# A dense expert stage cut in two: all U products first, their gelu parked in DRAM, then all sums over V

## The chip, the cores and the metric

The kernel runs on one core of one Trainium2 chip. The metric is device time in microseconds (us) of one execution. PE is the matrix engine, PEld its weight load, DVE the vector engine, ACT the scalar engine, POOL the GpSimd engine, SP the engine that only issues loads. "Row" below means one of the 128 slices of 128 experts, unless a row of the profile is meant.

## The reference, cut to what matters

A decoder block: a hybrid attention mixer on 16 meta tokens and 512 tokens, then a product-key expert layer (PEER), then a norm. The expert layer is what the change is about:

```python
s1 = jnp.einsum('thd,hkd->thk', q[:, :, 0], sub_keys1)      # 8 heads, 128 keys
s2 = jnp.einsum('thd,hkd->thk', q[:, :, 1], sub_keys2)
v1, i1 = lax.top_k(s1, 16); v2, i2 = lax.top_k(s2, 16)
cand = v1[..., :, None] + v2[..., None, :]
sc, pos = lax.top_k(cand, 16)                               # 16 of 256 pairs
eidx  = (i1 * 128 + i2) at pos                              # 8*16 experts a token
gates = softmax(sc)
act = gelu(einsum('nkd,nd->nk', expert_u[eidx], x), approximate=False)
y   = einsum('nk,nkd->nd', gates * act, expert_v[eidx])     # 16384 experts in all, d = 1024
```

## The kernel before

The 512 tokens are four blocks of 128. Blocks 0 to 2 go through `front(0)` and `mid(0)` (mixer and projections), block 3 through `front(1)` and `mid(1)`. `topk(b)` is the lookup of a block: on DVE, with a few score matmuls ahead of it.

For blocks 0 to 2 the expert layer is **dense**: all 16384 experts are computed, in 128 rows of 128 experts. `u_phase(i1)` loads a 512 KB slice of U (`uf`), splits it into a high part (ACT, `uh`) and a low part (DVE, `ul`), runs 24 matmuls of 384 columns into `pj`, and writes gelu of the result to a slot of `ring`, 24 slots in SBUF that earlier stages left free. `v_operands(i1)` loads a 512 KB slice of V (`vf`), splits it (`vh`, `vl`), multiplies the row's gelu with the gate table `gt` (line 986), splits that (`wh2`, `wl2`), and `v_block` adds 18 matmuls of 512 columns to six accumulators `acc`. The gate table comes from `spread(b)`: for each of the blocks 0 to 2 it builds one-hot matrices on DVE (`ohu`, `ohl`, `B`, lines 861 to 872) and POOL (`Am`), multiplies them on PE (`px`, 32 groups of four products a block, line 878), and stores the result to DRAM (`Gd`), from where `gt` is loaded for eight rows at a time.

Block 3 is **gathered**: for each of 128 pairs per token, POOL issues an indirect load of 128 expert rows from U (512 KB, `gu`), and DVE makes the dot product (`u_dot`, line 827); for each group of 16 pairs it then does the same from V (`v_sum`, line 838). That is 256 gathers and 256 DVE operations.

Two things set the order. A string, `SCHED`, names the steps up to the dense stage: `f` and `m` are steps of `front(1)` and `mid(1)`, `t`/`c` a lookup whole or its first step, `s` a spread, `u` an early U row. After it, U rows fill the ring; then one loop takes one U row (23 ahead) and one V row each pass, with lookup 3 and then `GRATE` = 2.35 gathered steps a pass. The order in the source is a priority; the framework's scheduler places the instructions on each engine, and each engine then runs in that order. U and V loads have two buffers each, gathers have five (`GB`).

## Time and profile before

| | us |
|---|---|
| median of 2 runs | 1719.8 (1718.99 to 1720.6) |
| the profiled execution, its own time | 1722.37 |
| its span, first to last instruction | 1720.6 |
| PE busy in the span | 1608.3 (93%) |
| DVE busy | 1233.7 (72%) |
| moved by DMA | 376.04 MB, mean 219 GB/s |

Sums are made against the span; the median lies 0.8 us below it, and the profiled execution's own time 1.8 us above. A busy PE counts matmuls from start to modelled end, which overlap, so "busy all the time" is read together with how far apart the matmuls start.

### The profile page before, as it was taken

The page shows a single profiled execution, that of the slowest core. Times are in us where ns is not written, and L with a number is a line of the kernel's source. Part 1 is how long each engine was busy: PE and PEld are TensorE (multiplying, and loading weights), DVE is VectorE, ACT ScalarE, POOL GpSimd, SP SyncE. Part 2 cuts the span into 40 slices and gives each one's busy share as a digit, 9 for nine tenths or more (in the row PEclk, how much of TensorE's full clock was granted, in tenths as well). Part 3 has the DMA queues.
Part 4 walks back from the last instruction along what each step waited for, and adds up shares of the span by engine and source line. Part 5 has one row for each costly group of instructions (what it writes and reads, how often), then busy time and mean ns, then how long its engine had stood idle before and what let it go on. Part 6 is the DMA issues. An engine that isn't in the chain of part 4 may idle for free.

```text
span 1720.6 us, 24532 instructions
## 1 busy us (share of the span) xinstructions
PE 1608.3 (93%) x9025; PEld 1432.2 (83%) x9025; DVE 1233.7 (72%) x2484; ACT 704.0 (41%) x1104; POOL 518.2 (30%) x401
## 2 busy tenths in 40 slices
PE   6998998977888789899999999999999999999996
PEld 6957988965577788899999999999999999999875
DVE  4225747489989888978777777777777777777664
ACT  5366365314445456333333333333333333333343
POOL 0020000003345455025334344343444433444310
PEclk9999999999899899999999999999999999999998
DMA  5202125342164345689887887987888888877654
GB/s 172 81 25 86 50 80 172 110 157 102 69 233 165 123 172 203 201 274 369 308 302 283 309 308 281 317 296 289 306 301 292 303 296 299 307 280 279 210 198 133
DMA packets 145705, 376.04 MB, mean 219 GB/s; under 512 B 13712, under 2 KB 63008, under 8 KB 142512
## 3 DMA queue, kind: packets, MB, share of 16 engines
q1 hardware_dynamic: 104112, 211.92, 37.1%
q0 software_dynamic: 36864, 134.23, 21.3%
q10 hardware_dynamic: 4608, 28.31, 4.1%
q8 instruction: 71, 1.16, 0.3%
q14 instruction: 50, 0.41, 0.1%
HBM read 345.03 MB, written 29.36 MB: 218 GB/s over the span
## 4 chain that ended last, share of the span: by engine, by line
PE 79%; DVE 13%; DMA 5%; ACT 2%; issue 1%; POOL 0%; SPq 0%; DVEq 0%; ACTq 0%; POOLq 0%
PE pj L187 12%; PE pj L189 12%; PE pj L188 12%; PE acc L188 9%; PE acc L189 9%; PE acc L187 9%; PE px L878 3%; DVE B L872 2%; PE pk L209 2%; PE pz L373 1%; PE pz L539 1%; DMA vf<-expert_v 1%; PE pz L525 1%; DVE sc L788 1%; DMA wf<-w_out 1%
## 5 line engine op out<-in xcount | busy, mean ns | idle before, releaser
L189 PE MATMUL pj<-xDh,ul 128*128 128x384 f32 x1000 | 338.5, 338 | 5.9 <-DVE ul L183 5.9
L188 PE MATMUL pj<-xDl,uh 128*128 128x384 f32 x1000 | 337.9, 338 | 0.0
L187 PE MATMUL pj<-xDh,uh 128*128 128x384 f32 x1000 | 337.8, 338 | 0.0
L188 PE MATMUL acc<-vl,wh 128*128 128x512 f32 x762 | 298.7, 392 | 1.5 <-DVE vl L183 1.5
L189 PE MATMUL acc<-vh,wl 128*128 128x512 f32 x762 | 298.6, 392 | 0.0
L187 PE MATMUL acc<-vh,wh 128*128 128x512 f32 x762 | 296.3, 389 | 0.4 <-ACT vh L182 0.4
L820 POOL DMA_INDIRECT gu<-expert_u,idx x128 | 183.2, 1431 | 334.4 <-DVE gu L827 193.0
L820 POOL DMA_INDIRECT gu<-expert_v,idx x128 | 178.1, 1392 | 279.3 <-DVE y L838 203.6
L182 ACT ACTIVATE uh<-uf 128x1024 fp32r<-128x1024 f32 x125 | 132.6, 1061 | 300.2 <-PE pj L188 253.6
L874 POOL TENSOR_TENSOR Am<-ohu,ohl 128x512 f32<-128x512 f32 x96 | 129.3, 1367 | 257.0 <-PE pz L530 152.4
L183 DVE TENSOR_TENSOR ul<-uf,uh 128x1024 fp32r<-128x1024 f32 x125 | 157.9, 1263 | 56.2 <-ACT uh L182 56.2
L189 PEld LDWEIGHTS pj<-xDh,ul 128*128 128x128 f32 x1000 | 189.3, 189 | 8.3 <-DVE ul L183 8.1
L187 PEld LDWEIGHTS pj<-xDh,uh 128*128 128x128 f32 x1000 | 189.1, 189 | 4.4 <-ACT uh L182 0.2
L188 PEld LDWEIGHTS pj<-xDl,uh 128*128 128x128 f32 x1000 | 189.3, 189 | 4.1
L188 PEld LDWEIGHTS acc<-vl,wh 128*128 128x128 f32 x762 | 143.0, 188 | 30.6 <-DVE vl L183 2.7
L189 PEld LDWEIGHTS acc<-vh,wl 128*128 128x128 f32 x762 | 143.0, 188 | 29.8
L187 PEld LDWEIGHTS acc<-vh,wh 128*128 128x128 f32 x762 | 143.0, 188 | 28.6 <-ACT vh L182 1.2
L838 DVE SCALAR_TENSOR_TENSOR y<-gu,act,y 128x1024 f32<-128x1024 f32 x128 | 163.8, 1279 | 0.5
L183 DVE TENSOR_TENSOR vl<-vf,vh 128x1024 fp32r<-128x1024 f32 x127 | 154.9, 1220 | 11.2 <-ACT vh L182 11.2
L827 DVE SCALAR_TENSOR_TENSOR gu<-gu,xn 128x1024 f32<-128x1024 f32 x128 | 154.6, 1218 | 0.0
L182 ACT ACTIVATE vh<-vf 128x1024 fp32r<-128x1024 f32 x127 | 133.1, 1048 | 21.1 <-DMA vf<-expert_v 19.8
L878 PE MATMUL px<-Am,B 128*128 128x128 f32 x768 | 102.7, 283 | 26.7 <-DVE B L872 17.1
(365 smaller groups left out, 2458.2 us busy)
## 6 DMA issues: line engine op xcount, KB each, us to landing
vf<-expert_v SPq DMA_DIRECT2D x128, 512.0 KB
uf<-expert_ut SPq DMA_DIRECT2D x125, 512.0 KB
wf<-w_in SPq DMA_DIRECT2D x48, 512.0 KB
Gd<-st ACTq DMA_DIRECT2D x24, 1024.0 KB
gt<-Gd SPq DMA_DIRECT2D x16, 1536.0 KB
wf<-w_out SPq DMA_DIRECT2D x16, 512.0 KB
wf<-w_pq SPq DMA_DIRECT2D x16, 512.0 KB
h<-x SPq DMA_DIRECT2D x4, 512.0 KB
```

What stands on the lines that cost most here:

```text
L182: A.activation(hi, src, AF.Copy)
L183: V.tensor_tensor(lo, src, hi.bitcast(F32), op=OP.subtract)
L187: T.matmul(outp, lh, rh, start=first, stop=False, skip_group_check=True)
L188: T.matmul(outp, lh, rl, start=False, stop=False, skip_group_check=True)
L189: T.matmul(outp, ll, rh, start=False, stop=last, skip_group_check=True)
L209: T.matmul(o, l, r, start=st, stop=sp, skip_group_check=True)
L820: P.indirect_dma_start(out=u, out_offset=None, in_=d[table], in_offset=bass.IndirectOffsetOnAxis(ap=col, axis=0))
L827: V.scalar_tensor_tensor(u, u, 1.0, xns[blk], op0=OP.mult, op1=OP.mult, accum_out=acts[blk][:, k:k + 1]))
L838: V.scalar_tensor_tensor(y, u, acts[blk][:, k:k + 1], y, op0=OP.mult, op1=OP.add))
L872: V.tensor_tensor(B, io4, iT[:, 1, c_].unsqueeze(2).to_broadcast(sh), op=OP.is_equal)
L874: P.tensor_tensor(Am.rearrange("p t (u l) -> p t u l", l=8), ohu[:, l_].unsqueeze(3).to_broadcast([128, 4, 16, 8]), ohl[:, l_].unsqueeze(2 ...
L878: T.matmul(p[:, j * 128:(j + 1) * 128], B[:, j], Am[:, j], start=True, stop=True)
```

## The change

All U rows now come first, then all V rows. The ring keeps rows 0 to 23; gelu of the other 104 rows goes, two rows to a 384 KB tile `ge` with four buffers, to a new DRAM tensor `Ad`, on ACT's queue, and is loaded again by SP ahead of the V row. U and V loads share the two buffers `uf` (and `uh`, `ul`). The lookups 1 to 3 and the three spreads leave `SCHED` and go into a queue that the U loop feeds at 0.75 of 4.3 us a row, with the yields' numbers as costs; when it is empty, the gathers follow at the same rate, and in the V loop at 0.45 of 4.3 us a row. A gathered step counts 1.3 us. Gathers get eight buffers. Spreads use four accumulator banks in turn instead of two.

```diff
-GB = 5
+GB = 8
+GEB = 4
-GRATE = 2.35
-TRATE = 16
-SCHED = "f f f u1 f f t0 c1 f f f f m s0 t1 c2 s1 u1 u1 t2 s2 m c3"
+RATES = (0.75, 0.45)
+SCHED = "f f f u1 f f t0 c1 f f f f m m"
...
+    Ad = drp.tile([NK // 2, 128, 2, ND * 128], F32, name="Ad")
...
     def u_phase(i1, early=False):
-        dst = ring_tile(i1 % len(ring))
+        nonlocal gp
+        if i1 < R:
+            dst = ring_tile(i1)
+        else:
+            if i1 % 2 == 0:
+                gp = du.tile([128, 2, ND * 128], F32, name="ge", bufs=GEB)
+            dst = gp[:, i1 % 2]
...
         A.activation(dst, pu, AF.Copy if early else AF.Gelu)
+        if i1 >= R and i1 % 2:
+            nc.scalar.dma_start(Ad[i1 // 2], gp)
...
     def v_operands(i1):
-        ge = ring_tile(i1 % len(ring))
-        vf = dp.tile([128, D], F32, name="vf", bufs=2)
+        if i1 < R:
+            ge = ring_tile(i1)
+        else:
+            if i1 % 2 == 0:
+                gp = du.tile([128, 2, ND * 128], F32, name="ge", bufs=GEB)
+                nc.sync.dma_start(gp, Ad[i1 // 2])
+            ge = gp[:, i1 % 2]
+        vf = du.tile([128, D], F32, name="uf", bufs=2)
...
-    for i1 in range(early, LA):
+    look = Queue(tks[1], part(tks[2]), spread(0, bp, bank2, 3), tks[2], part(tks[3]), spread(1, bp, bank2, 3), tks[3],
+                 spread(2, bp, bank2, 3))
+    for i1 in range(early, NK):
         u_phase(i1)
+        if look is not None:
+            look.run(4.3 * RATES[0])
+            if not look.jobs or i1 == NK - 1:
...
+                gen = gathered(3)
+                rows = Queue(gen)
+        else:
+            rows.run(4.3 * RATES[0])
...
     for i1 in range(NK):
-        if i1 + LA < NK:
-            u_phase(i1 + LA)
         last[i1] = v_operands(i1)
...
+        rows.run(4.3 * RATES[1])
```

Where the instructions stand now. First DVE, at the end of lookup 2 (`sc` and `sel` are the lookup's, `B`, `ohu`, `ohl`, `iT` a spread's, `ul` the low half of a U slice). Before:

```order
L788 SCALAR_TENSOR_TENSOR sc<-bb,fi 128x128 x6
L812 TENSOR_REDUCE sm<-gate_4503 128x8
L792 TENSOR_REDUCE sel_4504<-sc 128x128
L872 TENSOR_TENSOR B<-io_79,iT 128x512 x3
L813 RECIPROCAL sm<-sm 128x8
L872 TENSOR_TENSOR B<-io_79,iT 128x512
L814 TENSOR_TENSOR gate_4503<-gate_4503,sm 128x128
L872 TENSOR_TENSOR B<-io_79,iT 128x512 x3
L183 TENSOR_TENSOR ul<-uf,uh 128x1024 x2
L848 COPY iT<-px 128x384
```

The same place on DVE after the change:

```order
L186 TENSOR_TENSOR ul<-uf,uh 128x1024
L791 SCALAR_TENSOR_TENSOR sc<-bb,fi 128x128 x16
L817 TENSOR_TENSOR gate_4696<-gate_4696,sm 128x128
L795 TENSOR_REDUCE sel_4697<-sc 128x128
L186 TENSOR_TENSOR ul<-uf,uh 128x1024 x16
L877 TENSOR_TENSOR B<-io_80,iT 128x512 x2
L186 TENSOR_TENSOR ul<-uf,uh 128x1024
L877 TENSOR_TENSOR B<-io_80,iT 128x512
L865 TENSOR_TENSOR ohu<-io_80,iT 128x256
L868 TENSOR_TENSOR ohl<-io_80,iT 128x128
L870 TENSOR_TENSOR ohl<-ohl,iT 128x128
```

Lookups 1 and 2 still stand ahead of the U rows (the scheduler put them there, beside `front(1)` and `mid(1)`); five of the 96 `B` do too. The other 91 and lookup 3 stand between the `ul` of later U rows; the first gathered step comes behind the 87th `ul`.

Then DVE in the middle of the dense stage (`wl` is the low half of gelu times gate, `y` a gathered sum, `vl` the low half of a V slice, `oT0h` and `oT0l` are ring slots). Before:

```order
L183 TENSOR_TENSOR ul<-uf,uh 128x1024
L986 TENSOR_TENSOR oT0l<-oT0l,gt 128x384
L183 TENSOR_TENSOR wl_9971<-oT0h,wh_9970 128x384
L838 SCALAR_TENSOR_TENSOR y<-gu,act_93,y 128x1024
L183 TENSOR_TENSOR vl<-vf,vh 128x1024
L838 SCALAR_TENSOR_TENSOR y<-gu,act_93,y 128x1024
L183 TENSOR_TENSOR ul<-uf,uh 128x1024
```

After the change the same engine among the last U rows, where `gu` is a gathered dot product:

```order
L186 TENSOR_TENSOR ul<-uf,uh 128x1024
L830 SCALAR_TENSOR_TENSOR gu,act_94<-gu,xn_3900 128x1024 x2
L186 TENSOR_TENSOR ul<-uf,uh 128x1024
L830 SCALAR_TENSOR_TENSOR gu,act_94<-gu,xn_3900 128x1024 x3
L186 TENSOR_TENSOR ul<-uf,uh 128x1024
L830 SCALAR_TENSOR_TENSOR gu,act_94<-gu,xn_3900 128x1024 x2
```

And in the V loop, where `ul<-uf,uh` is the low half of a V slice:

```order
L186 TENSOR_TENSOR wl_10948<-oT0l,wh_10947 128x384
L841 SCALAR_TENSOR_TENSOR y<-gu,act_94,y 128x1024
L186 TENSOR_TENSOR ul<-uf,uh 128x1024
L186 TENSOR_TENSOR wl_10980<-oT0l,wh_10979 128x384
L841 SCALAR_TENSOR_TENSOR y<-gu,act_94,y 128x1024
L186 TENSOR_TENSOR ul<-uf,uh 128x1024
L841 SCALAR_TENSOR_TENSOR y<-gu,act_94,y 128x1024
L186 TENSOR_TENSOR wl_11015<-oT0l,wh_11014 128x384
L841 SCALAR_TENSOR_TENSOR y<-gu,act_94,y 128x1024
L186 TENSOR_TENSOR ul<-uf,uh 128x1024
```

Before, a pass had a U row, a V row and about two gathered steps; now a row alone has one or two. Counted over the whole order: 105 gathered steps stand among the last 40 U rows (2.6 a row), 151 among the first 100 V rows (1.51 a row), none in the last 28.

Last SP's queue of loads in the same place. Before:

```order
L971 DMA vf<-expert_v 128x1024
L931 DMA uf<-expert_ut 128x1024
L984 DMA gt<-Gd 128x24x128
L971 DMA vf<-expert_v 128x1024
L931 DMA uf<-expert_ut 128x1024
L971 DMA vf<-expert_v 128x1024
L931 DMA uf<-expert_ut 128x1024
```

After, in the V loop:

```order
L1003 DMA ge<-Ad 128x768
L1006 DMA uf<-expert_v 128x1024 x2
L1003 DMA ge<-Ad 128x768
L1006 DMA uf<-expert_v 128x1024
L1019 DMA gt<-Gd 128x24x128
L1006 DMA uf<-expert_v 128x1024
L1003 DMA ge<-Ad 128x768
L1006 DMA uf<-expert_v 128x1024 x2
```

Between two gate tables `gt` stand eight V loads and four reloads of gelu, where eight V and eight U loads stood.

## Rows read from the trace of the kernel before

**Rows 1.** The page, parts 1, 3, 5 and 6.

```profile
PE 1608.3 (93%) x9025; PEld 1432.2 (83%) x9025; DVE 1233.7 (72%) x2484; ACT 704.0 (41%) x1104; POOL 518.2 (30%) x401
...
q0 software_dynamic: 36864, 134.23, 21.3%
...
L183 DVE TENSOR_TENSOR vl<-vf,vh 128x1024 fp32r<-128x1024 f32 x127 | 154.9, 1220 | 11.2 <-ACT vh L182 11.2
L827 DVE SCALAR_TENSOR_TENSOR gu<-gu,xn 128x1024 f32<-128x1024 f32 x128 | 154.6, 1218 | 0.0
...
vf<-expert_v SPq DMA_DIRECT2D x128, 512.0 KB
...
gt<-Gd SPq DMA_DIRECT2D x16, 1536.0 KB
```

**Rows 2.** Windows: stretch, busy us per engine (instructions), PE clock, DMA share, GB/s.

```profile
330.00:735.00 405.00, 334.45 (x2221) 295.21 (x2221) 367.37 (x1277) 188.16 (x277) 139.96 (x104) 0.96 0.45 159
...
690.00:735.00 45.00, 39.36 (x209) 37.27 (x208) 43.18 (x211) 17.71 (x24) 0.00 (x0) 0.96 0.60 192
735.00:1604.00 869.00, 869.00 (x4399) 791.64 (x4398) 646.46 (x823) 305.36 (x425) 345.55 (x245) 1.00 0.85 299
1604.00:1650.00 46.00, 44.07 (x192) 35.37 (x191) 29.71 (x32) 15.53 (x21) 15.78 (x12) 1.00 0.71 239
1650.00:1690.00 40.00, 40.00 (x179) 33.11 (x178) 24.80 (x32) 18.19 (x29) 0.00 (x0) 1.00 0.46 152
780.00:800.00 20.00, 20.00 (x104) 18.34 (x103) 17.67 (x27) 7.78 (x11) 10.77 (x8) 1.00 1.02 401
785.00:795.00 10.00, 10.00 (x52) 8.98 (x51) 7.76 (x10) 5.34 (x8) 4.58 (x3) 1.00 1.02 409
```

**Rows 3.** Groups by line, DVE, 330 to 735: busy us, mean ns | idle before.

```profile
L872 DVE TENSOR_TENSOR B<-io,iT 128x512 f32<-128x512 f32 x96 | 88.5, 935 | 11.4 <-PE px L878 11.2
L183 DVE TENSOR_TENSOR ul<-uf,uh 128x1024 fp32r<-128x1024 f32 x20 | 29.4, 1472 | 2.7 <-ACT uh L182 2.7
L861 DVE TENSOR_TENSOR ohu<-io,iT 128x256 f32<-128x256 f32 x24 | 21.2, 885 | 1.9 <-POOL Am L874 1.9
...
L864 DVE TENSOR_TENSOR ohl<-io,iT 128x128 f32<-128x128 f32 x24 | 15.9, 664 | 0.0
...
L866 DVE TENSOR_TENSOR ohl<-ohl,iT 128x128 f32<-128x128 f32 x24 | 10.2, 426 | 0.2
```

**Rows 4.** Groups by line, PE, 330 to 735.

```profile
L878 PE MATMUL px<-Am,B 128*128 128x128 f32 x768 | 102.7, 283 | 26.7 <-DVE B L872 17.1 <-issue 5.6 <-POOL Am L874 3.3
```

**Rows 5.** Timeline of PE: start, us.

```profile
738.69 0.33 PE L189 MATMUL pj<-xDh,ul 128*128 128x384 f32 x1
...
741.81 0.33 PE L189 MATMUL pj<-xDh,ul 128*128 128x384 f32 x1
...
742.21 0.40 PE L187 MATMUL acc<-vh,wh 128*128 128x512 f32 x1
...
744.74 0.39 PE L189 MATMUL acc<-vh,wl 128*128 128x512 f32 x1
```

**Rows 6.** The chain that ended last, in order of time, 1600 to 1660: start, us.

```profile
1616.39 7.01 DMA vf<-expert_v
...
1625.85 4.71 DMA vf<-expert_v
...
1633.31 8.91 DMA vf<-expert_v
```

**Rows 7.** Timeline of ACT, first and last V split of the V-only stretch.

```profile
1609.27 1.05 ACT L182 ACTIVATE vh<-vf 128x1024 fp32r<-128x1024 f32 x1
...
1649.12 1.06 ACT L182 ACTIVATE vh<-vf 128x1024 fp32r<-128x1024 f32 x1
```

**Rows 8.** Timeline of PE, its last matmul.

```profile
1706.19 0.39 PE L189 MATMUL acc<-gu 128*128 128x512 f32 x1
```

More of the change, by code (lines that the diff above doesn't have):

```diff
@@ L752, in topk @@
                 if hh % 2 and s:
-                    yield
+                    yield 1.4
         for a0, na, nb_, off in SEGS:
@@ L770, in topk @@
                     V.max_index(i8[:, 8:], v8[:, 8:], x)
-            yield
+            yield 1.4
         fi = mp.tile([128, 2, NH, TK], F32, name="fi")
@@ L854, in spread @@
         V.tensor_copy(iT[:, 3], ii[:, 1])
+        yield 1.5
         sh = [128, 4, 128]
@@ L866, in spread @@
             V.tensor_tensor(ohl, ohl, iT[:, 2, tc_].unsqueeze(2).to_broadcast([128, TT, 8]), op=OP.mult)
+            yield 1.2
             for t4 in range(TT // 4):
@@ L880, in spread @@
                              p.rearrange("p (t i) -> p t i", t=4), AF.Copy)
+                yield 1.0
             nc.scalar.dma_start(Gd[128 // TT * DENSE.index(blk) + tb], st)
@@ L900, in build, with __init__, run @@
     tks = {b: topk(b) for b in range(4)}
+    class Queue:
+        def __init__(self, *jobs):
+            self.jobs, self.owed = list(jobs), 0.0
+        def run(self, us):
+            self.owed += us
+            while self.jobs and self.owed > 0:
+                c = next(self.jobs[0], None)
+                if c is None:
+                    self.jobs.pop(0)
+                else:
+                    self.owed -= c
+            if not self.jobs:
+                self.owed = 0.0
     ring = []
@@ L907, in build @@
         ring += [None] * n
-    LA = len(ring) - 1
-    acc = gt = dp = None
+    R = len(ring)
+    acc = gt = dp = gp = None
     uname = {}
@@ L952, in build @@
                 early += 1
-        else:
-            tags = itertools.cycle(("px", "pk") if st[0] == "S" else ("px",))
-            spread(int(st[1]), bp, lambda: bank(next(tags)), 3)
     for _ in f1:
@@ L976, in v_operands @@
         else:
-            vh = dp.tile([128, D], F32R, name="vh", bufs=2)
-            vl = dp.tile([128, D], F32R, name="vl", bufs=2)
+            vh = du.tile([128, D], F32R, name="uh", bufs=2)
+            vl = du.tile([128, D], F32R, name="ul", bufs=2)
             wh = dp.tile([128, ND * 128], F32R, name="wh2", bufs=2)
@@ L1007, in gathered @@
                     u_dot(blk, k)
-                    yield
+                    yield 1.3
                 weights(blk, slice(hh * TK, (hh + 1) * TK))
@@ L1012, in gathered, with part @@
                     v_sum(blk, y, k)
-                    yield
-    for i1 in range(early, LA):
-        u_phase(i1)
-    pool_close("bld")
+                    yield 1.3
+    def part(gen, n=1):
+        for c in itertools.islice(gen, n):
+            yield c
+    tags = itertools.cycle(("px", "pk"))
+    bank2 = lambda: bank(next(tags))
+    look = Queue(tks[1], part(tks[2]), spread(0, bp, bank2, 3), tks[2], part(tks[3]), spread(1, bp, bank2, 3), tks[3],
+                 spread(2, bp, bank2, 3))
+    gb = gen = rows = None
+    for i1 in range(early, NK):
+        u_phase(i1)
+        if look is not None:
+            look.run(4.3 * RATES[0])
+            if not look.jobs or i1 == NK - 1:
+                look.run(1e9)
+                look = None
+                pool_close("bld")
+                pool_close("mid")
+                gb = ctx.enter_context(tc.tile_pool(name="gat", bufs=1, reuse_waits="tile"))
+                gen = gathered(3)
+                rows = Queue(gen)
+        else:
+            rows.run(4.3 * RATES[0])
     dp = ctx.enter_context(tc.tile_pool(name="dn", bufs=1, reuse_waits="tile"))
@@ L1032, in build @@
                 v_block(i1, i, ops)
-        if gb is None:
-            for _ in range(TRATE):
-                if next(tks[3], 1) == 1:
-                    pool_close("mid")
-                    gb = ctx.enter_context(tc.tile_pool(name="gat", bufs=1, reuse_waits="tile"))
-                    gen = gathered(3)
-                    break
-        else:
-            done += GRATE if i1 + LA < NK else GRATE / 2
-            while done >= 1:
-                next(gen, None)
-                done -= 1
+        rows.run(4.3 * RATES[1])
     for _ in gen:
@@ L1072, in build @@
     for i, blk in enumerate(DENSE):
[L1073 removed]
+        hb = du.tile([128, D], F32, name="uh", bufs=2)
         nc.sync.dma_start(hb, hd[blk])
```

10 lines of the change are left out of this document (4 added, 6 removed).

## The prediction

> **What bounds the kernel now.** I read the page first, then the windows, then the groups of the one stretch where PE is not the bound, then the tail. PE is busy 93% of the span [rows 1], and from 735 to 1604 it is busy every microsecond [rows 2]: nothing that is only moved inside that stretch can help. Its pace there comes from two starts of the timeline [rows 5]: 18 U matmuls from 738.69 to 741.81, 0.173 us each, so 24 x 0.173 = 4.16 us a U row; 11 V matmuls from 742.21 to 744.74, 0.23 us each, so 18 x 0.23 = 4.1 us a V row. What can be won lies in 330 to 735: PE is busy 334.5 of 405 us, DVE 367.4 [rows 2]. There DVE does lookups and spreads, and PE has too little that is ready. What can be lost lies in DMA: before, it moves 299 GB/s through the long stretch [rows 2], with U, V and gathers spread evenly over it.
>
> **Part one: from 330 to the first U row.** Nothing ahead of 330 moves. The order shows that lookups 1 and 2 still run ahead of the U rows, so DVE remains the bound there. From its 367.4 us go the spreads, 88.5 + 21.2 + 15.9 + 10.2 = 135.8, the U splits, 29.4 [rows 3], and lookup 3, which ran in 690 to 735: DVE is busy 43.2 there [rows 2], some of it U splits, so I take 38 (30 to 43). 164 us stay. Five of 96 `B` with their helpers stay too, 5/96 of 135.8 = 7, and DVE was idle for 405 - 367.4 = 38 us, of which I keep 9, since most of that idle time belongs to the spreads' exchange with PE and POOL. U rows start near 330 + 164 + 7 + 9 = 510. Bounds: 490 with no waits, 530 if `front(1)` and `mid(1)`, which lose the spreads as company, wait more for their own loads and norms.
>
> **Part two: U rows beside the spreads.** 87 rows at 4.16 are 362 us. 91 spread groups come on top on PE: 102.7 us busy for 96 [rows 4] is 1.07 with its waits, so I take 1.0, 91 us. Where lookup 3 and spread 1 fall together DVE needs a little more than PE; 10 us for that, estimated from a lookup's 38 us over a spread's 45 us and some dozen splits at 1.22 [rows 1], against a dozen rows and 32 groups of PE. DMA has room here. End: 510 + 463 = 973 (945 to 1000).
>
> **Part three: the last 40 U rows, with 2.6 gathers each.** A U load is 512 KB, which is 0.524 MB [rows 1]; a gather is 134.23/256 = 0.524 MB [rows 1]; the stored gelu is 0.197 MB a row. Together 0.524 + 0.197 + 2.6 x 0.524 = 2.08 MB. In 4.16 us that would be 500 GB/s. The most that the trace shows is 401 over 20 us and 409 over 10 us [rows 2]. DVE runs in order, with the dot products ahead of the next row's `ul`, so a late gather holds the split, and PE behind it. At 401 a row lasts 5.19 us; eight buffers instead of five only shift that by a few gathers. I add 0.15 for loads that collide and take 5.35: 214 us. Bounds 5.09 (at 409) and 6.0. DVE itself, a split and 2.6 dot products at 1.22 us [rows 1], needs 4.4 us and is not the last to end.
>
> **Part four: V rows.** The direct evidence is the end of before, where the U rows are used up and V rows run alone with little over one gather each (POOL's 12 instructions in 46 us [rows 2]). From 1609.27 to 1649.12 [rows 7] nine V rows take 39.85 us, 4.43 each, 0.33 more than PE needs, and PE falls to 44.07 of 46 busy while DMA moves only 239 GB/s [rows 2]. The chain says why: it runs through V loads that landed 7.01, 4.71 and 8.91 us after the split that freed their buffer [rows 6]. Two buffers at 4.1 us a row leave 8.2 us for load, ACT's copy and DVE's split; the latter two take 1.05 [rows 7] and 1.22 [rows 1], so a load that needs over 5.9 us makes PE wait. In the long stretch the same two buffers had twice the row time. After the gathers, from 1650, PE is full again [rows 2].
> The changed V loop is that tail, longer and heavier. Its first 24 rows move 0.524 + 1.51 x 0.524 + a share of the gate table (1536 KB for eight rows [rows 1], 0.197) = 1.51 MB: the tail's 4.43, 106 us. The next 76 reload gelu as well, 1.71 MB, 4.26 us at 401 GB/s, already over PE's 4.1; with the tail's 0.33 it is 4.6, 350 us (4.18 to 5.2). The last 28 have no gathers: 4.1 each, 115, and about 2 us for each of three gate tables ahead of V loads in SP's queue, 121 in all. From the last matmul to the end of the span are 1720.6 - 1706.2 = 14 us [rows 8], unchanged.
>
> **What is hidden.** The gelu's copy in and out costs ACT nothing new but two issues per row pair; the store stands behind its own gelu. Multiplying gelu by gate moves ahead for the ring's rows only. POOL's issue of gathers overlaps DMA. Each of these stays off the path as long as DMA ends last.
>
> **Sum.** 973 + 214 + 106 + 350 + 121 + 14 = **1778** of span, against 1720.6; the median lay 0.8 below the span, which I leave out. That is 3.4% slower: some 40 us won ahead of the gathers (PE's idle time of 70 us in 330 to 735, less what the lookups keep), and 100 lost behind, because a dense stage that had its DMA spread evenly now has 256 gathers in its second half with half the time for each load.
>
> **Rivals.**
> *PE alone decides.* If gathers and loads always land in time, it is 973 + 40 x 4.16 + 128 x 4.1 + 14 = 1678, 2.4% faster. For it speaks that PE lost nothing in 780 to 800 at 401 GB/s [rows 2]. Against it: part three would need 500 GB/s, which no stretch reaches. It decides only if the gathers in flight can absorb 0.9 us a row over 40 rows. Chance 0.06.
> *DMA's rate decides, without late loads.* At 409 GB/s throughout: 973 + 40 x 5.09 + 24 x 4.1 + 76 x 4.18 + 28 x 4.1 + 14 = 1722, no change. For it: nothing ahead in time of the tail shows a late V load, and the tail's waits are few. Against it: the tail waited at 239 GB/s, so rate is not what made it wait. Chance 0.29. The Trainium skill ("DMA: Bandwidth & Descriptors", section "Queues, rings and completion order") says that each DMA engine takes turns between the queues that have work, a packet at a time. By that rule a U or V load would get its turn beside any number of gathers, and this rival's 1722 would be the time. The rows of the tail, 8.91 us at 239 GB/s, speak against it.
> *The gate table blocks V loads.* A `gt` of 1.57 MB is issued on the same SP queue ahead of V loads, every eight rows; at 401 GB/s it alone takes 3.9 us, and the two-buffer slack of the V loop is used up by then. 16 of them add 63: 1841. In before it had twice the time and PE did not wait in 735 to 1604 [rows 2]. Chance 0.13.
>
> The Trainium skill, in the section "Bandwidth" of "DMA: Bandwidth & Descriptors", gives some 358 GB/s as a core's share of the memory, which would make the heavy rows 5.82 and 4.78 us and the sum 1799. The trace shows 401 over 20 us, so the sum does not use it.
>
> **Chances and range.** A measurement of this kernel tells about 2% from no change, 34 us. Forecast (1755 to 1840) 0.52, rate alone 0.29, gate table 0.13, PE alone 0.06. Uncertain ends of part one and two, 25 us either way, go in. Range 1710 to 1845. Faster by over 2% (under 1685): 0.06; within: 0.29; slower: 0.65.
>
> **What would show it.** U rows start near 510 and follow at 4.2 us with PE full until the queue is empty, near 973, and DMA low there. Then DMA goes to 390 or more, DVE's dot products wait for gathers, and U rows take over 5 us. In the V loop rows take 4.4 to 4.7 us with ACT's `vh` copy (now named `uh`) waiting for its load, until the gathers end; the last 28 rows are back at 4.1. Wrong would be: U rows with gathers at 4.2 us (then DMA carries more than it ever showed), V rows with gathers at 4.1, or a start of U far from 510.

## The result and the profile after

The changed kernel takes 1948.3 us (median of 2 runs, 1946.32 to 1950.29) against 1719.8: 1.1329 times as long, interval [1.1274, 1.1383]. Forecast were 1778 with a range up to 1845. The direction was right, the size was not: of 228 us lost, 57 were foreseen. The profiled execution has a span of 1948.5 us.

The page of the changed kernel, parts 1, 3 and 5, answers [rows 1]:

```profile
PE 1669.6 (86%) x9025; PEld 1457.9 (75%) x9025; DVE 1234.0 (63%) x2484; ACT 712.8 (37%) x1110; POOL 532.0 (27%) x401
...
q0 software_dynamic: 36864, 134.23, 18.1%
...
L186 DVE TENSOR_TENSOR ul<-uf,uh 128x1024 fp32r<-128x1024 f32 x254 | 311.3, 1226 | 329.1 <-ACT uh L185 327.3
```

In the changed kernel `ul` is the low half of U and of V slices. Before, those of V were `vl` [rows 1], and those of U had a line of their own (page, part 5, before):

```profile
L183 DVE TENSOR_TENSOR ul<-uf,uh 128x1024 fp32r<-128x1024 f32 x125 | 157.9, 1263 | 56.2 <-ACT uh L182 56.2
```

DVE does the same work as before (1234.0 us in the same 2484 instructions), POOL issues the same gathers, and PE has the same 9025 matmuls. What is new is waiting: DVE stood still for 329.1 us ahead of the low halves, nearly all of it (327.3) until ACT's high half was there. Before, it was 56.2 us ahead of `ul` and 11.2 ahead of `vl`, 67.4 together.

Windows of the changed kernel, columns as in [rows 2]; the stages follow from the first regular U row's gelu at 540, the first gather near 1000, the last U row near 1268 and the last gather at 1780:

```profile
330.00:400.00 70.00, 55.48 (x433) 47.02 (x433) 56.63 (x306) 16.89 (x50) 0.00 (x0) 0.99 0.47 151
400.00:540.00 140.00, 95.38 (x481) 70.54 (x480) 109.21 (x540) 49.70 (x85) 16.88 (x13) 0.82 0.25 83
540.00:1000.00 460.00, 444.70 (x2815) 440.45 (x2815) 278.73 (x497) 214.40 (x270) 150.15 (x93) 0.99 0.51 176
1000.00:1268.00 268.00, 202.79 (x1049) 189.65 (x1049) 187.92 (x241) 63.75 (x93) 148.26 (x111) 0.90 0.97 365
1268.00:1780.00 512.00, 424.77 (x1691) 331.35 (x1689) 359.16 (x477) 142.49 (x193) 198.33 (x143) 0.93 0.87 303
1780.00:1915.00 135.00, 130.65 (x561) 106.21 (x562) 77.78 (x105) 50.72 (x72) 1.51 (x1) 0.99 0.59 188
1100.00:1125.00 25.00, 19.74 (x106) 17.81 (x105) 22.77 (x26) 8.32 (x12) 15.02 (x13) 1.00 1.03 411
1250.00:1260.00 10.00, 0.00 (x0) 0.00 (x0) 0.06 (x1) 1.15 (x2) 0.00 (x0) 0.61 0.86 293
```

Read the PE column against the length of each stretch. Ahead of 1000 PE is idle 14.5 + 44.6 + 15.3 = 74.4 us; before, it was idle 405 - 334.5 = 70.6 in 330 to 735 [rows 2]. So the move of lookups and spreads filled no idle time of PE: most of it now lies in 400 to 540. Behind 1000 PE is idle 65 us of 268 and 87 of 512, and in 1250 to 1260 it does nothing at all, while DMA still moves 293 GB/s: something is being moved, but not what PE waits for.

What that is, SP's queue of the changed kernel shows (timeline: start, duration of the issue, operation; entries of one kind in a row are put together, with the whole stretch as the duration):

```profile
1234.86 0.38 SPq L1019 DMA_DIRECT2D gt<-Gd  x1
1238.22 13.94 SPq L960 DMA_DIRECT2D uf<-expert_ut  x1
...
1298.48 0.38 SPq L1019 DMA_DIRECT2D gt<-Gd  x1
1301.23 28.14 SPq L1006 DMA_DIRECT2D uf<-expert_v  x5
1329.98 0.38 SPq L1019 DMA_DIRECT2D gt<-Gd  x1
1333.13 4.41 SPq L1006 DMA_DIRECT2D uf<-expert_v  x2
```

ACT's timeline of the same place, where the bracket is the idle time ahead of the instruction and its releaser:

```profile
1301.65 1.07 ACT L185 ACTIVATE uh<-uf 128x1024 fp32r<-128x1024 f32 x1 [0.26 <-DMA uf<-expert_v]
...
1317.27 1.06 ACT L185 ACTIVATE uh<-uf 128x1024 fp32r<-128x1024 f32 x1 [11.53 <-DMA uf<-expert_v]
...
1346.54 1.06 ACT L185 ACTIVATE uh<-uf 128x1024 fp32r<-128x1024 f32 x1 [8.09 <-DMA uf<-expert_v]
```

And the chain of waits, whose rows 1301 and 1333 are those two loads:

```profile
1161.08 21.19 DMA uf<-expert_ut
...
1301.23 15.94 DMA uf<-expert_v
...
1333.13 13.31 DMA uf<-expert_v
```

These three loads, each asked for right behind a gate table `gt`, took 13 to 21 us, against the 4.7 to 8.9 of [rows 6]. It is not one accident. SP asks for the first eight tables at 1009, 1022, 1157, 1235, 1298, 1330, 1434 and 1479; U rows, by the starts of their gelu on ACT, have gaps of 16.3, 21.5, 19.1 and 18.9 us from 1015, 1031, 1164 and 1241 on, and V rows have gaps of 15.6, 12.3, 14.6 and 12.9 from 1302, 1334, 1437 and 1483 on. Such a gap of two or more rows' time is called a hole below. Behind each of the next seven tables, asked for from 1522 to 1792, there is one too, of 8.0 to 14.5 us; behind the last, asked for at 1824, when the gathers are over, the longest gap is 7.2. From 1053 to 1164, between two holes, U rows take 5.1 us.

The spreads beside U (groups by line, DVE, 330 to 1000), and the last matmul, answer [rows 3] and [rows 8]:

```profile
L877 DVE TENSOR_TENSOR B<-io,iT 128x512 f32<-128x512 f32 x96 | 110.5, 1178 | 15.0 <-PE px L883 11.8 <-PE pk L883 3.2
```

```profile
1926.82 0.39 PE L192 MATMUL acc<-gu 128*128 128x512 f32 x1
```

### The profile page after: what moved, and what is told of

It reads as the page before. It is cut to its first block, busy times and chain, and to the rows that moved or that the text cites. A ratio compares the mean times of both kernels' runs of the same rounds, so it can differ in the third digit from the quotient of the medians.

```text
span 1948.5 us, 24683 instructions
## 1 busy us (share of the span) xinstructions
PE 1669.6 (86%) x9025; PEld 1457.9 (75%) x9025; DVE 1234.0 (63%) x2484; ACT 712.8 (37%) x1110; POOL 532.0 (27%) x401
## 2 busy tenths in 40 slices
DMA packets 160682, 416.94 MB, mean 214 GB/s; under 512 B 15377, under 2 KB 64673, under 8 KB 157489
## 4 chain that ended last, share of the span: by engine, by line
PE 47%; DMA 21%; DVE 17%; issue 8%; ACT 4%; POOL 2%; SPq 0%; DVEq 0%; ACTq 0%; POOLq 0%
PE pj L190 8%; PE pj L192 8%; PE pj L191 8%; DMA uf<-expert_v 8%; DMA ge<-Ad 6%; PE acc L191 4%; PE acc L192 4%; PE acc L190 4%; DMA uf<-expert_ut 3%; DVE ul L186 3%; POOL gu L823 2%; PE pk L212 2%; DVE y L841 2%; DVE wl L186 2%; PE pk L883 1%
## 5 line engine op out<-in xcount | busy, mean ns | idle before, releaser
L186 DVE TENSOR_TENSOR ul<-uf,uh 128x1024 fp32r<-128x1024 f32 x254 | 311.3, 1226 | 329.1 <-ACT uh L185 327.3
L185 ACT ACTIVATE uh<-uf 128x1024 fp32r<-128x1024 f32 x254 | 267.9, 1055 | 530.7 <-PE pj L191 218.3
L191 PE MATMUL acc<-ul,wh 128*128 128x512 f32 x762 | 313.1, 411 | 44.3 <-DVE ul L186 43.9
L190 PE MATMUL acc<-uh,wh 128*128 128x512 f32 x762 | 307.9, 406 | 46.3 <-ACT uh L185 46.3
L192 PE MATMUL acc<-uh,wl 128*128 128x512 f32 x762 | 307.1, 403 | 0.9 <-DVE wl L186 0.9
L879 POOL TENSOR_TENSOR Am<-ohu,ohl 128x512 f32<-128x512 f32 x96 | 154.5, 1630 | 379.7 <-PE pk L883 187.6
L191 PEld LDWEIGHTS acc<-ul,wh 128*128 128x128 f32 x762 | 149.6, 196 | 95.0 <-DVE ul L186 63.8
L190 PEld LDWEIGHTS acc<-uh,wh 128*128 128x128 f32 x762 | 149.1, 196 | 83.8 <-ACT uh L185 51.8
L192 PEld LDWEIGHTS acc<-uh,wl 128*128 128x128 f32 x762 | 149.4, 196 | 32.3 <-DVE wl L186 1.6
L830 DVE SCALAR_TENSOR_TENSOR gu<-gu,xn 128x1024 f32<-128x1024 f32 x128 | 153.9, 1219 | 11.0 <-DMA gu<-expert_u,idx 11.0
L185 ACT ACTIVATE wh<-ge 128x384 fp32r<-128x384 f32 x103 | 53.9, 523 | 260.6 <-PE acc L191 251.6
L877 DVE TENSOR_TENSOR B<-io,iT 128x512 f32<-128x512 f32 x96 | 110.5, 1178 | 15.0 <-PE px L883 11.8
```

The lines of the kernel that those rows point to most:

```text
L185: A.activation(hi, src, AF.Copy)
L186: V.tensor_tensor(lo, src, hi.bitcast(F32), op=OP.subtract)
L190: T.matmul(outp, lh, rh, start=first, stop=False, skip_group_check=True)
L191: T.matmul(outp, lh, rl, start=False, stop=False, skip_group_check=True)
L192: T.matmul(outp, ll, rh, start=False, stop=last, skip_group_check=True)
L830: V.scalar_tensor_tensor(u, u, 1.0, xns[blk], op0=OP.mult, op1=OP.mult, accum_out=acts[blk][:, k:k + 1]))
```

## The experiments

Three explanations stood against each other after the result. **G**: a gate table holds up the loads that stand behind it on SP's queue. **R**: the bytes of a row at the highest rate that DMA reaches set the pace. **P**: the gelu that was parked in DRAM comes back late. Later a fourth was added, **H**: DVE's multiply of gelu by gate, moved ahead in its order, takes the slack of the loads. Beside the whole time, V's pace compares the runs: PE instructions in the window 1300 to 1700 over 18 give the V rows in 400 us. (In all runs of the table PE does nothing but V rows in that stretch. How many gathers fall into it differs from run to run, so small differences of pace mean little.) Ratios are to the kernel before, measured again beside each run.

| run | median us | ratio to before | V row us | PE busy of 400 |
|---|---|---|---|---|
| changed kernel | 1948.3 | 1.133 [1.127, 1.138] | 5.45 | 331.8 |
| tables on ACT's queue | 1883.7 | 1.095 [1.089, 1.100] | 4.85 | 360.9 |
| tables in eight slices | 1858.8 | 1.079 [1.074, 1.084] | 4.92 | 358.1 |
| tables in 12 KB pieces | 1894.6 | 1.104 [1.096, 1.111] | 5.08 | 349.4 |
| gelu not parked | 1910.5 | 1.110 [1.104, 1.117] | 5.26 | 339.1 |
| even gathers, 1.52 a row | 1926.9 | 1.120 [1.113, 1.127] | 5.29 | 337.3 |
| five gather buffers | 1960.7 | 1.142 [1.129, 1.154] | 5.50 | 327.4 |
| the same and four load buffers | 1920.7 | 1.115 [1.112, 1.118] | 5.07 | 347.0 |
| multiply held in its row | 1948.9 | 1.136 [1.127, 1.145] | 5.63 | 321.8 |
| no gathers, new place of lookups | 1754.7 | 1.020 [1.014, 1.026] | 4.27 | 389.2 |
| no gathers, place as before | 1753.6 | 1.021 [1.014, 1.028] | 4.26 | 388.9 |
| all mended, old place | 1759.8 | 1.026 [1.022, 1.029] | 4.25 | 390.1 |

**Where the tables stand.** The first edit only changes the queue that asks for the table:

```diff
-            nc.sync.dma_start(gt, Gd[:, :, i1:i1 + IC, :].rearrange("a p i t -> p a i t"))
+            nc.scalar.dma_start(gt, Gd[:, :, i1:i1 + IC, :].rearrange("a p i t -> p a i t"))
```

> Only the queue of the 16 gate-table loads (1536 KB each) changes, from SP's to ACT's. Theory G (U and V loads stand behind a gate table in SP's queue: four holes of 16 to 22 us among the U rows, some ten of 9 to 15 us among the V rows): most of the holes go, 1948 becomes 1780 to 1850. Theory R (the bytes per row are more than DMA can move): the bytes are the same, 1930 to 1960. Theory P (the reload of gelu is what V rows wait for): no change either.

1883.7, 65 us better, but above G's range. Most of V's holes are gone (three of 8 to 10 us are left), but three U holes of 20 to 26 us stay. ACT's timeline of that run shows why:

```profile
1010.51 0.71 ACTq L1019 DMA_DIRECT2D gt<-Gd  x1
...
1018.59 21.04 ACTq L967 DMA_DIRECT2D Ad<-ge  x1
1039.73 0.49 ACT L965 ACTIVATE ge<-pj 128x384 f32<-128x384 f32 x1 [20.11 <-issue]
```

The store of gelu at 1018.59 took ACT 21.04 us to issue, instead of 0.33, behind the tables asked for on the same queue at 1006 and 1010, and everything that ACT computes stood behind it. Two more such issues, at 1154 and 1234, took 9.5 and 10.4 us. In this run the queue that holds the tables is the one that suffers. In the changed kernel it was SP's own issue that was held, for 13.94 us at 1238.22 above. The second edit leaves the table on SP, in eight parts (`gate_part` loads three of the 24 blocks), one behind each V load; not shown: both loads are held in program order:

```diff
-        if i1 % IC == 0:
-            gt = dp.tile([128, TB, IC, TT], F32, name="gt", bufs=2)
-            nc.sync.dma_start(gt, Gd[:, :, i1:i1 + IC, :].rearrange("a p i t -> p a i t"))
+        if i1 % IC == 0:
+            gt = gtn
+            if i1 + IC < NK:
+                gtn = dp.tile([128, TB, IC, TT], F32, name="gt", bufs=2)
+        if i1 // IC * IC + IC < NK:
+            gate_part(gtn, i1 // IC * IC + IC, i1 % IC)
```

> The gate table of eight V rows is loaded in eight slices of 192 KB, one behind each V load on SP's queue, instead of in one piece of 1536 KB; the first table's eight slices still come in one lump ahead of the first V row. Bytes and order of the rest unchanged. Theory G (a whole gate table holds up the loads behind it on SP's queue): the holes of 9 to 15 us every eight V rows go, V rows with gathers take 4.8 instead of 5.4 us, as with the tables on ACT's queue; the U stretch keeps about one hole of 20 us instead of four, since only the first table and one slice a row are asked for there; 1830 to 1870 in all. Theory R (DMA's rate alone sets the row time): the bytes are the same, so 1930 to 1950. Theory P (the reloaded gelu is what is late): unchanged, 1930 to 1950.

1858.8, as G had it, with the same bytes; by R nothing should have changed. Two things moved along with the slices, though. The first part of a table is asked for at 1210 only, so the U stretch holds none: its last matmul starts at 1219 instead of 1267, 48 of the 90 us. And the multiply by the gate stands mostly one to four rows ahead of its row on DVE, where the changed kernel has it five to seven ahead. So this run alone doesn't tell the lump from the multiply in V rows. The U stretch keeps holes of 11 and 10 us, and is now bound by rate (window of that run, U rows with gathers):

```profile
1010.00:1200.00 190.00, 166.72 (x881) 154.66 (x881) 156.93 (x198) 52.65 (x77) 140.73 (x101) 0.97 1.02 409
```

881 matmuls are 36.7 rows of 24 in 190 us, 5.18 each: the 5.19 that the prediction worked out from 401 GB/s. The third edit keeps queue, place and size of the table and turns its layout in DRAM, so that a partition's share is one piece of 12 KB and not 24 of 512 B (not shown: the store during the spreads is turned with it):

```diff
-    Gd = drp.tile([TB, 128, 128, TT], F32, name="Gd")
+    Gd = drp.tile([NK // IC, 128, TB, IC * TT], F32, name="Gd")
...
-            nc.sync.dma_start(gt, Gd[:, :, i1:i1 + IC, :].rearrange("a p i t -> p a i t"))
+            nc.sync.dma_start(gt.rearrange("p a i t -> p a (i t)"), Gd[i1 // IC])
```

> The gate table's layout in DRAM is turned, so that its load reads one piece of 12 KB for each partition instead of 24 pieces of 512 B, and its store, during the spreads, writes the 512 B pieces. Queue, place, bytes, and number of loads as in the changed kernel. Theory G with pieces (a table takes 11 to 26 us because each of its 3072 pieces takes a turn): holes shrink to the 4 us that its bytes need, U and V: 1840 to 1880. Theory G by bytes alone (1.57 MB in one lump ahead of the loads, whatever its pieces): holes stay, 1930 to 1950. Theory R: 1930 to 1950.

1894.6: 54 us better, between the two forms of G. One U hole of 18.4 us (at 1014), smaller ones up to 9.5, and V holes of 8 to 11 stay. This is the cleanest of the three runs: SP, ACT, DVE and POOL do the same in the same order as in the changed kernel, and the first gather starts at 993 us instead of 994, so the turned store costs nothing ahead of it. The size of the load's pieces alone is worth the 54 us. That the rest of the hole is the lump's bytes is argued, not shown.

**The rate and the parked gelu.** First one rate for all gathers, beside U and beside V:

```diff
-            rows.run(4.3 * RATES[0])
+            rows.run(4.3 * 0.46)
...
-        rows.run(4.3 * RATES[1])
+        rows.run(4.3 * 0.46)
```

> The gathers at one rate over all rows behind the spreads, 1.52 a row (2.6 and 1.51 before). Theory R: U rows go from 5.1 to about 4.3 us, 30 us, and the last V rows get slower by some 10: about 1925 to 1930. Theory G: holes among the U rows shrink with the gathers, from 16 to about 12 us, and there are more of them among the last V rows: 1925 to 1945. Neither expects a way back to 1720.

Then store and reload left out; the four tiles `ge` are used in turn by both loops:

```diff
-        if i1 >= R and i1 % 2:
-            nc.scalar.dma_start(Ad[i1 // 2], gp)
...
-                nc.sync.dma_start(gp, Ad[i1 // 2])
```

> Leaves out the store of gelu and its reload (104 rows); V rows use four stale tiles instead, so the result of blocks 0 to 2 is not the reference's. 41 MB less. Theory P: DVE's 75 us of waits for gelu go and with them as much time, 1860 to 1880. Theory G: the holes stay, 1900 to 1935. Theory R: V rows at 1.51 MB instead of 1.71, 0.5 us each, 76 of them: about 1905.

1926.9 and 1910.5. Evening out the gathers is worth 21 us, which both G and R had expected. Leaving the parking out is worth 38, in G's range and not in P's. Neither removes the holes: single edits show R and P as small. Third, no gathers at all, and none of DVE's 256 operations on them (block 3 gets no expert sum):

```diff
-        for hh in range(NH + 1):
+        yield 1.3
+        for hh in range(0):
```

> Leaves out all 256 gathers and their DVE operations, so block 3 gets no expert sum; all else is the same. Theory G: a gate table alone in the DMA lands in some 7 us and holds a V load by about 3, so about 1700 to 1750. Theory R: all of the loss behind the spreads goes, 1700 to 1715 (U starts at 540, spreads until 1000, 40 x 4.16 + 128 x 4.1 + 14). Theory P: V rows still wait for gelu, over 1760.

1754.7, 5 us above G's range. So 194 us of the changed kernel's time need the gathers and their DVE operations as company; what is left is still 35 us slower than the kernel before, which has its gathers.

**The place of lookups and spreads.** The steps go back into the string, where `s` runs a spread whole; 256 gathers then fit beside U:

```diff
-SCHED = "f f f u1 f f t0 c1 f f f f m m"
+SCHED = "f f f u1 f f t0 c1 f f f f m s0 t1 c2 s1 u1 u1 t2 s2 m c3"
...
-    look = Queue(tks[1], part(tks[2]), spread(0, bp, bank2, 3), ..., spread(2, bp, bank2, 3))
+    look = Queue(tks[3])
```

> Lookups and spreads go back to where the kernel before has them, ahead of the dense rows; all else stays as changed (all U first, parked gelu, eight row buffers, gathers at the same rates, now from the 19th U row on, so that all 256 lie in U rows). If moving lookups and spreads beside U is worth the 40 us that the prediction gave it, this costs 40 on one side; if it is worth about 5 us, as the count of rows at equal times in the two traces says, it costs 5. Theory R: 2.5 gathers a row over 105 U rows take 5.1 us a row, V rows without gathers 4.2, so 735 + 105 x 5.1 + 128 x 4.2 + 14 = 1822. Theory G adds its holes in V rows only where something else is in flight beside the tables: without gathers some 3 us each, 16 of them, 1870 at most. Theory P has the gelu reloads late also without gathers: V rows at 4.6 or over, 1873 or more.

1906.8, above the sum by R, 1822, and above G's most, 1870. Its U rows with 2.5 gathers each take 250 x 24 / 1212 = 4.95 us at 408 GB/s, the most over 250 us that any run shows from 500 us on (window):

```profile
1050.00:1300.00 250.00, 228.26 (x1212) 208.63 (x1211) 211.06 (x230) 72.56 (x104) 178.21 (x125) 0.99 1.02 408
```

What this run loses among its U rows is five holes of 12.7 to 20.0 us (from 744, 763, 848, 924 and 1000 on), one behind each of five tables, asked for at 738, 743, 840, 917 and 993: the multiplies pull the tables among the gathers again. Without gathers beside them its V rows take 4.3 us on average, 4.08 in most rows, and behind each table there is one row of 6.5 to 8.2: a table without gathers costs little, but not nothing.

```diff
-            rows.run(4.3 * RATES[0])
+            rows.run(4.3 * 0.33)
...
-        rows.run(4.3 * RATES[1])
+        rows.run(4.3 * 0.33)
```

> As the run with the old front, but the gathers at one even rate of 1.1 a row over U and V rows, as the kernel before spreads them. Theory R: every row then moves under 1.3 MB, no row is bound by rate, U and V rows take 4.2 us: 735 + 105 x 4.2 + 128 x 4.25 + 14 = 1734, near the kernel before. Theory G: 14 of 16 tables are loaded while gathers run and cost 9 to 12 us each on top: 1860 to 1900. Theory P: V rows at 4.6 for the 104 parked ones: 1775.

1892.9 with 1.1 gathers a row everywhere: behind the first five tables, which are over by 800, U rows run at 4.16 and have no hole; V rows take 5.1 and have a hole of 8 to 12 for nearly each table. The rate in the V stretch is only 280 GB/s, so this is G without R. The value of the place itself was then measured without gathers and their DVE operations. The first of two runs has the old place, but lookup 3 earlier than in the kernel before; the second, whose difference from the first is shown, has it behind the 23rd U row:

> Lookups and spreads ahead of U as in the kernel before, and all 256 gathers and their vector operations left out (block 3 gets no expert sum); set against the run that leaves the gathers out with the new place of lookups and spreads, 1754.7. If moving lookups and spreads beside U won 30 to 40 us, as the prediction had it, this run is slower by that, 1785 to 1795. If the move won nothing because front and mid of block 3 lost their company, and the first gate table then stands in the way of U rows at 1000, this run is faster: 735 + 105 x 4.16 + 128 x 4.22 + 14 = 1726.

```diff
-            look.run(4.3 * RATES[0])
+            if i1 >= R - 1 and None in [next(tks[3], None) for _ in range(8)]:
+                look.jobs.clear()
```

> All 256 gathers and their vector operations left out (block 3 gets no expert sum); lookups and spreads ahead of U, and lookup 3 behind the 23rd U row as in the kernel before. Beside 1754.7 for the new place and 1767.8 for the old one with lookup 3 interleaved earlier. If the old place is as good as the new once lookup 3 stands right, 1735 to 1750; if the new place wins what the prediction gave it, 1785 and over; if lookup 3's place is worth nothing, 1765.

1767.8 and 1753.6. Against 1754.7 for the new place: the move is worth nothing that these runs could tell, where 40 us were forecast. Lookup 3's place may be worth the other 14; that is at the edge of what two runs each can tell.

**More buffers.** Four buffers for the loads of U and V slices; gathers give up three to make room, so the first line runs alone as well:

```diff
-GB = 8
+GB = 5
...
-            uf = du.tile([128, KT, 128], F32, name="uf", bufs=2)
+            uf = du.tile([128, KT, 128], F32, name="uf", bufs=4)
```

> Four buffers for the loads of U and V slices instead of two, and five gather buffers instead of eight to make room. If the holes are loads that come late behind a gate table and two buffers are too few to ride over it, two more rows of 4.2 to 5 us of slack cover most of a hole of 9 to 20 us: 1820 to 1860. Theory R: bytes unchanged, fewer gathers in flight: 1930 to 1960. Theory P: the gelu tiles keep four buffers, unchanged: 1930 to 1960.

> The changed kernel with five gather buffers instead of eight, nothing else. If the 28 us of the run with four load buffers came from the load buffers, this is 1945 to 1960. If they came from having fewer gathers in flight beside the loads, 1915 to 1930.

1920.7 with both lines, 1960.7 (1952.3 to 1969.1) with the first alone: the two load buffers give some 40 us, far less than G had expected, 1820 to 1860. In V rows of 1300 to 1700 ACT hardly waits for V loads any more (11.7 us against 86.5), but another wait took its place (waits of the run with four load buffers, 1300 to 1700: engine and line, what it waited for, total us, times, longest):

```profile
DVE ge L1021 <- DMA ge<-Ad: 75.4, 27, 7.7
PEld acc L191 <- DVE ul L186: 64.5, 29, 6.8
```

**Together, and what was still missing.** Old place and 1.1 gathers a row with, first, one slice a row and four load buffers, second, the 12 KB pieces:

> All suspects at once: lookups and spreads where the kernel before has them, gathers at 1.1 a row over all rows, gate tables in eight slices, four load buffers and five gather buffers. If what the two-phase order loses is only G and R, this comes to the count of rows: 735 + 105 x 4.16 + 128 x 4.25 + 14 = 1730 to 1760, the kernel before. If something else is lost (the reloaded gelu, P, or the loads' time at twice the pace), V rows stay at 4.7 or more: 1800 and over.

> Old place of lookups and spreads, gathers at 1.1 a row, and the gate table with 12 KB pieces, two load buffers and eight gather buffers. Beside the run with the same order and small pieces, 1892.9, in which V rows take 4.9 to 5.4 us. Theory G with pieces: V rows 4.3 to 4.5, 1760 to 1790. Theory G by bytes, or P: 1880 to 1900.

1845.5 and 1852.8, both above what G had expected, 1730 to 1760 (with R) and 1760 to 1790. Not the sum of the parts: V rows still take 4.8 us. In the first, holes came every eight rows; a slice that waits for its table's buffer at the head of SP's queue was suspected, and the slices moved to rows 4 to 7. The first of two runs has two more differences, lookup 3 behind the 23rd U row and 1.2 gathers a row; the second has lookups and spreads beside U, as in the changed kernel, and 1.52 gathers a row:

```diff
-        if i1 // IC * IC + IC < NK:
-            gate_part(gtn, i1 // IC * IC + IC, i1 % IC)
+        if i1 // IC * IC + IC < NK and 3 <= i1 % IC <= 6:
+            if i1 % IC == 3:
+                gtn = dp.tile([128, TB, IC, TT], F32, name="gt", bufs=2)
+            for j in range(2):
+                gate_part(gtn, i1 // IC * IC + IC, (i1 % IC - 3) * 2 + j)
```

> As the run with all suspects at once, 1845.5, with three differences: the eight slices of the next gate table are asked for two at a time in rows 4 to 7 of the table in use, by when its buffer has long been free, instead of one in each row from the first; lookup 3 stands behind the 23rd U row as in the kernel before, and gathers follow at 1.2 a row. If the rest of the loss is the slice that waits for its buffer at the head of the queue (once in eight rows), V rows fall from 4.8 to 4.2 to 4.4: 1745 to 1790. If the two-phase order by itself costs it (every V row now needs two loads at twice the pace beside gathers), 1820 to 1850.

> The same slices, load and gather buffers with lookups and spreads beside U as in the changed kernel, and gathers at one rate of 1.52 a row behind the spreads. If only the tables' place in the queue costs time, 1755 to 1790, as without gathers. Theory R: 1.6 to 1.7 MB a row at 401 GB/s are 4.2 us and a little more, 1780 to 1820, above the run with the old place, because 256 gathers have 168 rows instead of 215. If the two-phase order costs it by itself: 1850 and over.

1860.0 and 1930.5: that suspicion was wrong, for the V rows did not get faster (5.25 and 5.46 us). The second, with slices and four load buffers, is no faster than even gathers without either, 1926.9, and has a hole of 10 to 17 us for each table again. In its window 1300 to 1700 the multiply on DVE waited 47.5 us for reloaded gelu and 20.4 for parts of the table: parts that are asked for late are late for a multiply that stands rows ahead. So it seems that slices help only if they come before the multiply wants them; no run tested that alone. The waits of the first run, 1300 to 1700, name the same pair as above:

```profile
DVE ge L1037 <- DMA ge<-Ad: 79.5, 24, 7.3
PEld acc L191 <- DVE ul L186: 69.5, 25, 6.8
```

DVE's order in the changed kernel tells the reason. In a V row (`ge_11284` is the gelu of two rows, `ge_11493` that of the two rows three tiles later):

```
1089 L1021 TENSOR_TENSOR ge_11493<-ge_11493,gt_11432 128x384
1090 L186 TENSOR_TENSOR wl2_11291<-ge_11284,wh2_11290 128x384
1091 L830 SCALAR_TENSOR_TENSOR gu_11315,act3_94<-gu_11315,xn3_3900 128x1024
1092 L186 TENSOR_TENSOR ul_11289<-uf_11286,uh_11288 128x1024
1093 L1021 TENSOR_TENSOR ge_11493<-ge_11493,gt_11432 128x384
1094 L186 TENSOR_TENSOR wl2_11323<-ge_11284,wh2_11322 128x384
```

The multiply by the gate stands three tiles, five to seven rows, ahead of the row that uses it, in all of the V loop behind the ring's rows. Four tiles hold eight rows, so one to three rows are left for the reload's trip, and DVE, which runs in order, waits there with the row's own low half behind it. The edit holds the multiply behind the same row's low half. (The expectation below puts it there in the kernel before as well. That is not so: counted on its DVE, 21 more multiplies than V splits have run in the middle of the dense stage. There the gelu stays in the ring, and no reload is waited for.)

```diff
-        V.tensor_tensor(g3, g3, gt[:, :, i1 % IC, :], op=OP.mult)
+        tc.keep_in_program_order(V.tensor_tensor(g3, g3, gt[:, :, i1 % IC, :], op=OP.mult))
```

> The changed kernel with one difference: each row's multiply of gelu by the gate table is held on DVE behind the low half of the same row's V slice, where the kernel before has it, instead of up to six rows ahead. Theory H (the multiply that was moved ahead makes DVE wait for tables and gelu long before they are needed, and lets four tables into the U stretch instead of two): two of the four U holes go, 35 to 40 us, the multiplies' wait of 60 us for reloaded gelu in V rows goes, and what is left are V loads late behind the tables: 1850 to 1890. Theory G alone (the loads behind a table are late, whoever asks): the number of tables is the same, 1920 to 1950.

> The run with late slices, four load buffers, the old place of lookups and spreads and 1.2 gathers a row, 1860.0, with the multiply held in its row. If that order was the rest of the loss, V rows fall from 5.1 to 4.2 to 4.4, and it ends near the run without gathers, 1753.6: 1755 to 1790. If the reload itself is late in its own row too, or the V loads, 1830 to 1860.

Alone it gives nothing, 1948.9, as G alone had expected: H by itself falls. Two U holes went, since only two tables are asked for in the U stretch (1008 and 1023, the third at 1277), but the tables moved into V rows, and there the held multiply now passes each late V load on to PE (waits of this run, 1300 to 1700):

```profile
ACT wh L185 <- DVE ge L1021: 108.3, 45, 3.5
PEld acc L190 <- ACT wh L185: 92.3, 34, 10.3
ACT uh L185 <- DMA uf<-expert_v: 86.3, 22, 11.0
```

On top of late slices, four load buffers, even gathers and the old place it takes 100 us away: 1759.8, inside the range expected. The run without it is the one whose late slices suit an early multiply badly; against the earlier run with one slice a row, 1845.5, the gain is 86. Windows of the kernel without the held multiply and, below, with it:

```profile
1300.00:1700.00 400.00, 340.82 (x1372) 272.00 (x1371) 267.05 (x364) 113.28 (x156) 140.83 (x90) 0.93 0.83 293
```

```profile
735.00:820.00 85.00, 85.00 (x489) 85.00 (x489) 49.09 (x67) 28.98 (x41) 23.74 (x21) 1.00 0.78 274
1300.00:1700.00 400.00, 390.13 (x1693) 314.72 (x1692) 332.21 (x434) 149.97 (x196) 167.65 (x102) 1.00 0.98 350
```

94 V rows in place of 76, at 350 GB/s instead of 293, and no wait of an engine for a transfer is among the longest seven. With all 256 gathers it ends 6 us behind the run of the same place without them, 1753.6, which has none of the other edits; the changed kernel ended 194 behind its own. A version that beats the kernel before did not come out of this: the best complete one, 1759.8, is 2.6% slower.

## Why the prediction was wrong

By its own steps, on the profiled execution; the terms below, 30, -3, 54, 82 and 8, sum to 171; the span missed by 170.5, the rest is rounding. The step that failed is the gate table: it was priced at nothing among the U rows and at 2 us in three places among the V rows, and its holes account for nearly all of parts three and four.

- **Part one**, U rows near 510: they came at 540, 30 us late and 10 beyond the bound. DVE's work was right: 165.8 us busy in 330 to 540 against the 171 of the sum. Its idle time was not: I had kept 9 of 38 us, and it stood still for 44. In 400 to 540 PE is busy 95 of 140 us at a granted clock of 0.82, a mean of stretches at its two levels (1.2 and 2.4 GHz), DVE 109, and the chain runs through loads of `w_out` and `w_pq` and the steps of `front(1)` and `mid(1)`. That fits the reason named for the bound of 530, lost company; no run tested it.
- **Part two**: 460 us against 463. Right.
- With them fell the sum's **"some 40 us won ahead of the gathers"**: PE's idle time is 74.4 instead of 70.6, and the two runs without gathers, old place and new, differ by 1 us.
- **Part three**, 40 U rows at 5.35: 268 us from 1000 to 1268 instead of 214, 54 more. The rate was right, 5.1 us a row between holes and 5.18 at 409 GB/s with sliced tables. What was missing: four tables were asked for there, each with a hole of 16 to 21 us, 76 together, where four rows at 5.35 would have taken 21: that is the whole of the 54. I had placed no table in this part at all, because "multiplying gelu by gate moves ahead for the ring's rows only" was listed as hidden. 21 of the multiplies for the ring's 24 rows run among the U rows, empty the table buffers early, and so pull four tables forward.
- **Part four**, V rows: 659 us (1268 to 1927) instead of 577, 82 more. The tail's 4.43 and 4.6 a row, taken from a stretch without tables, became 5.45 in 1300 to 1700. This is where the failed step cost most. **The gate table** stood among the rivals with a chance of 0.13, at 3.9 us a table, its bytes at 401 GB/s, added to the forecast: the right mechanism at too low a price, and kept out of the sum but for three tables. Eleven tables in fact had holes of 8 to 16 us there, 130 together. The other rows took 4.55 us on average, where 577 is 4.51 a row; so the holes cost 80 more than eleven such rows, nearly all of the 82. Experiments on the table itself gave back part of the loss of U and V rows: slices 90 us, another queue 65, longer pieces alone 54. Why not more: behind the tables stand further waits, for late loads, where two more buffers were worth some 40, and for reloaded gelu.
- The sentence on the **multiply** was false beyond the ring as well: five to seven rows ahead throughout. Holding it gave nothing alone, and 86 to 100 us on top of slices, load buffers, even gathers and the old place.
- **Tail**: 1948.5 - 1926.8 = 22 us instead of 14, 8 more. "Unchanged" overlooked the last edit of the change: the first two final loads of `hd` now go to the two buffers `uh`, which the last V matmuls read, and no longer to `vf`. They are asked for at 1925.9 and 1926.6, beside the last matmul at 1926.8; before, at 1696.3 and 1698.2, with 10 and 8 us to go to the last matmul at 1706.2.
- **The rivals.** "PE alone decides", 1678, was not reached even with no gathers at all (1754.7). "DMA's rate decides" describes U rows between holes, and nothing else: V rows moved 299 GB/s in 1300 to 1700, less than the 350 at which the mended kernel runs without a hole. The Trainium skill's turn between queues ("DMA: Bandwidth & Descriptors", section "Queues, rings and completion order") was used for loads against gathers. The turn says nothing for loads against what stands ahead of them on their own queue, and that was what counted. An estimate by that rule, with 512 B of table for each 4 KB of gather, would even let a table of 3072 pieces last some (512 + 4096) x 3072 B / 401 GB/s = 35 us if gathers never run out, and the run with 12 KB pieces agrees in direction (54 us less). The estimate counts each piece as one packet, and so does the profile: the page of the changed kernel's profile has 64673 - 15377 = 49296 packets of 512 B to 2 KB, and 16 tables have 49152 pieces.

Not tried: the mended V loop with lookups and spreads beside U and the multiply held. V rows stay at 4.25 us on average instead of 4.1, for two different reasons by the traces: without gathers most rows take 4.08, and one or two behind each table 4.8 to 8.2; in the mended kernel no row in 1300 to 1700 takes over 4.9, but about one in four takes 4.5 to 4.9. What makes the latter is open, and so is which of the mended kernel's five edits could be left out.

## What to carry to other kernels

A transfer on a queue can cost those behind it far more than its bytes at the best rate, here a hole of 8 to 21 us for what is 3.9 us at 401 GB/s: look at what is queued behind the largest one, and cut it, lengthen its pieces, or ask for it early enough for whoever waits first. When a stage loses its second kind of work, every wait that this work had covered comes due at once, and mending one of them only shows the next; single edits gave 0 to 90 us here, and the last one, worthless alone, 86 to 100. Before counting on a filled hole, compare an engine's idle time up to the same point of the work, not its idle time in one stretch.

## What the runs showed of the hardware

- An engine that issues a transfer can be held by its queue: ACT's issue of a store took 21.04 us behind two tables of 3072 pieces each, otherwise 0.33; SP's issue of a U load took 13.94 us behind one. The Trainium skill ("DMA: Bandwidth & Descriptors", section "Issuing engines are not separate DMA queues") says that issuing from several engines saves only the time of the issue; here the queue of the table decided who waited, and the change of queue alone was worth 65 us.
- The size of a load's pieces mattered beside gathers: the same 16 tables in pieces of 12 KB instead of 512 B, with the same order on SP, ACT, DVE and POOL, took 54 us off the kernel.
- DMA kept 408 GB/s over 250 us with gathers and 512 KB loads.
- The same `B` comparison on DVE took 1178 ns beside U rows against 935 before [rows 3], and POOL's `Am` 1630 against 1367. The reason was not studied.
